# Weights in contiguous slices, prepared in halves, and the rotary product taken from PSUM, in a two-layer attention trunk

## The chip, the core and the metric

The kernel runs on one core of a Trainium2 chip. The metric is the time of one execution in microseconds of device time; the median of three runs is what a change is judged by. The core's engines are PE (matrix multiply), DVE (VectorE), ACT (ScalarE), POOL (GpSimd) and SP (SyncE, which here only issues transfers). Each takes its own instructions strictly in the order in which the program emits them, and waits on semaphores for the others.

## The reference

The input is x, 1024 tokens by 1024 features in float32. Layer A and layer B each add a block to the residual stream, with an RMS norm before and after the block:

```python
# layer A: 16 heads of 64, each query chunk of 64 sees its own and 8 previous chunks
u = rmsnorm(h, a_norm_pre);  q, k, v, g = split(u @ a_w_in, 4)      # 1024 x 4096
o = chunk_band_attention(q, k, v, positions, rel_bias)              # softmax(qk/8 + bias) v
h = h + rmsnorm((o * silu(g)) @ a_w_out, a_norm_post)
# shared keys and values, projected once from the stream
ks, vs = split(rmsnorm(h, kv_norm) @ kv_w, 2);  ks = partial_rope(ks)  # 1024 x 2048
# layer B: 8 heads, two softmax maps each, block-causal
q, g = split(rmsnorm(h, b_norm_pre) @ b_w_in, 2);  q = partial_rope(q)
a = softmax(q0 k0) - lam * softmax(q1 k1)
o = rmsnorm(a @ v, b_subln) * (1 - lam_init)
h = h + rmsnorm((o * silu(g)) @ b_w_out, b_norm_post)
```

partial_rope turns the first 16 of each 64 features: t * cos + swapped(t) * sin.

## The kernel before

**Arithmetic.** Every float32 matrix product is made of three passes over rounded operands: high weights by high data, high weights by low data, low weights by high data. So each operand is cut: a cast gives its high part (`hi_of`, on ACT), a subtraction its low part (`lo_of`, on DVE). A projection group (`mm_group`, L265, L267, L269) is 24 matrix products of 128x128 by 128x512 into one PSUM tile `acc`, of which there are two.

**Order.** Nothing is scheduled by a planner: the class `Ticks` writes the order out by hand. A tick emits first what was put `at` it, then four matrix products of the running stream (`program`), then what was put `after` it or `later`, by rank (0 first) and then by when it was put there. `later(k, f, rank)` means k ticks after the present one, and the rank is 1 where none is given. A projection group takes 6 ticks, and a head pair u takes 8 groups, 48 ticks, in the order `ORDER`: keys and queries of tokens 0 to 511 (K0, Q0), those of tokens 512 to 1023 (K1, Q1), then V0, G0, V1, G1 for values and gates. The attention of pair u begins 24 ticks after the pair's first group and takes 6 ticks for each block of 128 queries in layer B. So blocks 4 to 7 of one pair run beside K0, Q0, K1 and Q1 of the next.

**An attention block in layer B** (`attB_block`): t0 emits the first map's scores (PE L595, one PSUM buffer `sp`), with the mask and the minimum by DVE (`red`, L604, rank 0); t0 + 1 the exponential on ACT (L610); t0 + 3 and t0 + 4 the same for the second map; t0 + 6 the combination of the two maps (`mix`, DVE L936, L937, L939), which stands behind the first `red` of the next block on DVE; t0 + 8 and t0 + 9 transposes on PE (L166, `tp<-ident,s`), each cut by ACT (same tick) and DVE (next tick, rank 0); t0 + 12 and t0 + 13 the product with the values (L970). `close` follows: `c4` (DVE L989) waits for a reciprocal root on POOL.

**The rotary part** (`rope`, L875) is called in the last tick of a K or Q group, which is one tick ahead of the next block's t0. In that tick ACT copies `acc` to `xs` (L883) and SP issues four small transfers from `xs` to `w`, the swapped features. At +2 POOL multiplies `xs` by the cosines in place (L889), at +3 it multiplies `w` by the sines (L890); at +6 DVE adds the two (L891); at +7 ACT makes the high part (L190) and at +8 DVE the low part (L193); for queries SP then sends the parts to the other half of the partitions (L518).

**Weights.** Layer A (`Weights`): ACT issues the load of a 512 KB slice of 128 columns (L216), POOL copies it to its high part (L202), DVE subtracts at the next tick. Layer B's 32 slices are prepared while layer A runs (`Prepared.prepare`, L231): every 10.5 ticks ACT issues a load (L235), at +4 POOL multiplies by the norm's gain (L243), at +6 ACT makes the high part, at +7 DVE the low part, and at +9 SP stores both to DRAM (`wcut`). Loads of weights read 128 columns of a row-major matrix, so each partition's 4 KB come in eight pieces of 512 bytes.

**Output stage of a layer** (`out_stream`): for each of 8 token tiles two groups of 24 products (L780); `finish` computes the norm's factor at its tick, the residual `hres` by DVE at +1 (L813), and in layer A at +2 `next_norm` (`more`): ACT squares and sums `hres` (L186), POOL takes the root, ACT scales (L1026), and PE transposes the tile 8 and 10 ticks later (6 and 7 for the last tile).

Of the kernel before, what the change touches and what calls it, by code (L numbers as in the profile page):

```python
# [11 lines left out]
F32 = mybir.dt.float32  # L12
# [4 lines left out]
ALU = mybir.AluOpType  # L17
# [5 lines left out]
D = 1024  # L23
P = 128
NT = S // P
NC = D // P
# [80 lines left out]
def trunk(ctx, tc, x, positions, a_norm_pre, a_w_in, a_rel_rev, a_w_out, a_norm_post,  # L107
# [5 lines left out]
    adma = nc.scalar.dma_start  # L113
    K = Ticks()
# [4 lines left out]
    o2 = out[0]  # L119
    w_in_a = a_w_in[0].rearrange("(c p) n -> p c n", p=P)  # L120
    w_out_a = a_w_out[0].rearrange("(c p) n -> p c n", p=P)
    w_kv = kv_w.rearrange("(c p) n -> p c n", p=P)
    w_in_b = b_w_in[0].rearrange("(c p) n -> p c n", p=P)
    w_out_b = b_w_out[0].rearrange("(c p) n -> p c n", p=P)
# [64 lines left out]
    def hi_of(src, hi):  # L189
        A.copy(out=hi, in_=src)  # L190
# [9 lines left out]
    def w_split(w):  # L200
        hi, lo = w_tile("whi"), w_tile("wlo")
        G.tensor_scalar(out=hi, in0=w, scalar1=1.0, scalar2=1.0, op0=ALU.mult, op1=ALU.mult)  # L202
        K.later(1, lambda: lo_of(w, hi, lo), 2)
        return hi, lo

    class Weights:
# [5 lines left out]
        def load(self, k, queue=adma):  # L212
            if k < len(self.specs) and k not in self.raw:
                view, cols = self.specs[k]
                self.raw[k] = w_tile("wst").bitcast(F32)
                queue(out=self.raw[k], in_=view[:, :, cols:cols + P])  # L216

# [7 lines left out]
    class Prepared:  # L225
# [5 lines left out]
        def prepare(self, k):  # L231
            view, cols, gain = self.specs[k]
            w = mp.tile([P, D], F32, tag="h", name="w", bufs=4)
            w3 = w.rearrange("p (c n) -> p c n", n=P)
            adma(out=w3, in_=view[:, :, cols:cols + P])  # L235

            def cut():
                hi = mp.tile([P, D], F32, tag="h", name="wh", bufs=4)
                K.later(0, lambda: hi_of(w, hi.bitcast(F32R)))
                K.later(1, lambda: lo_of(w, hi.bitcast(F32R), w.bitcast(F32R)), 2)  # L240
                K.later(3, lambda: [dma(out=wcut[k][:, 0, :], in_=hi), dma(out=wcut[k][:, 1, :], in_=w)])

            K.later(4, lambda: G.tensor_tensor(out=w3, in0=w3, in1=gain.unsqueeze(2).broadcast_to([P, NC, P]),  # L243
                                               op=ALU.mult))
            K.later(6, cut)

# [90 lines left out]
    x_load(1)  # L337
    WA = Weights([(w_in_a, kc * D + u * P) for u in range(8) for kc in (1, 0, 2, 3)])
    WA.load(0, dma)
# [466 lines left out]
    def finish(t, first, second, h, dst, more):  # L806

        def a():
# [9 lines left out]
            if more is not None:  # L818
                K.later(2, lambda: more(t, h))

# [54 lines left out]
    def rope(acc, half, then):  # L875

        cs = slice(half * 512, (half + 1) * 512)
        xs = lp.tile([P, 512], F32, tag="px", name="xs", bufs=3)
        w = rot[swc[0] % 2]
        swc[0] += 1  # L880
# [7 lines left out]
        K.later(0, a)  # L888
        K.later(2, lambda: G.tensor_tensor(out=xs, in0=xs, in1=rot["cos"][:, cs], op=ALU.mult))  # L889
        K.later(3, lambda: G.tensor_tensor(out=w, in0=w, in1=rot["sin"][:, cs], op=ALU.mult))  # L890
        K.later(6, lambda: V.tensor_tensor(out=xs, in0=xs, in1=w, op=ALU.add))  # L891
        then(xs, 6 + 1)

# [12 lines left out]
    def attB(u, base):  # L906
        par = u % 2
        for i in range(NT):
            attB_block(u, par, i, base + 6 * i)

# [112 lines left out]
    def next_norm(t, h):  # L1023
# [3 lines left out]
        for cg in range(2):  # L1027
            K.at(K.pos + (6 + cg if t == NT - 1 else 8 + 2 * cg), lambda cg=cg: transposed(z, cg, uT_dst(R2, t)))

    WB = Prepared([(w, off + u * P, gn) for u in range(8)  # L1030
                   for w, off, gn in ((w_kv, 0, kvg), (w_in_b, 0, bng), (w_kv, D, kvg), (w_in_b, D, bng))])
    OA, OB = OutTiles(otA), OutTiles(otB)
# [147 lines left out]
```

## Time and profile before

| | us |
|---|---|
| median of three runs (1332.06 to 1335.57) | 1332.92 |
| the profiled execution | 1333.15 |
| its span, first to last instruction | 1331.0 |
| PE busy in the span | 1289.9 |
| DVE busy | 834.6 |
| ACT busy | 662.3 |
| POOL busy | 540.2 |

The profiled execution is 2.15 us longer than its span. Engines overlap, so their times do not add up. PE's busy time counts matrix products with modelled ends. Layer A's projections and attention run to about 565 us of the span, its output stage to 689, layer B's projections and attention to about 1200, its output stage to the end.

### The profile page before, as it was taken

The page shows a single profiled execution, that of the slowest core. Times are in us where ns is not written, and L with a number is a line of the kernel's source. Part 1 is how long each engine was busy: PE and PEld are TensorE (multiplying, and loading weights), DVE is VectorE, ACT ScalarE, POOL GpSimd, SP SyncE. Part 2 cuts the span into 40 slices and gives each one's busy share as a digit, 9 for nine tenths or more (in the row PEclk, how much of TensorE's full clock was granted, in tenths as well). Part 3 has the DMA queues.
Part 4 walks back from the last instruction along what each step waited for, and adds up shares of the span by engine and source line. Part 5 has one row for each costly group of instructions (what it writes and reads, how often), then busy time and mean ns, then how long its engine had stood idle before and what let it go on. Part 6 is the DMA issues. An engine that isn't in the chain of part 4 may idle for free.

```text
span 1331.0 us, 20601 instructions
## 1 busy us (share of the span) xinstructions
PE 1289.9 (97%) x6919; PEld 1088.3 (82%) x6919; DVE 834.6 (63%) x1712; ACT 662.3 (50%) x1462; POOL 540.2 (41%) x718
## 2 busy tenths in 40 slices
PE   5999999999999999999998999999999999999998
PEld 5888888888888887887877888888888888888886
DVE  5568866967565655675333575757575757578643
ACT  4355574566454545563343454545454545456311
POOL 2266656656555655542223242424242424242311
PEclk8999999999999999999999999999999999999999
DMA  6588777777877777663464232323232323225353
GB/s 214 137 252 250 243 243 235 228 220 232 250 238 216 241 212 250 194 214 104 142 206 118 71 108 75 109 74 109 74 109 74 104 80 104 79 77 172 98 153 104
DMA packets 160917, 213.46 MB, mean 160 GB/s; under 512 B 13952, under 2 KB 114336, under 8 KB 160800
## 3 DMA queue, kind: packets, MB, share of 16 engines
q1 hardware_dynamic: 83616, 138.08, 33.9%
q10 hardware_dynamic: 77184, 73.95, 18.1%
q8 instruction: 57, 0.93, 0.3%
q14 instruction: 60, 0.49, 0.1%
HBM read 136.47 MB, written 59.79 MB: 147 GB/s over the span
## 4 chain that ended last, share of the span: by engine, by line
PE 52%; DVE 2%; issue 1%; ACT 1%; POOL 1%; DMA 1%; SPq 0%; ACTq 0%; DVEq 0%; POOLq 0%
PE acc L780 12%; PE acc L265 9%; PE acc L267 9%; PE acc L269 9%; PE sp L595 5%; PE av L970 4%; PE tp L166 4%; DVE R L193 1%; DMA sw<-xs 1%; PE av L697 0%; DVE s L604 0%; DVE hres L813 0%; DVE s L939 0%; POOL s L649 0%; ACT R L190 0%
## 5 line engine op out<-in xcount | busy, mean ns | idle before, releaser
L269 PE MATMUL acc<-R,wlo 128*128 128x512 f32 x1008 | 410.7, 407 | 0.0
L267 PE MATMUL acc<-R,whi 128*128 128x512 f32 x1008 | 404.3, 401 | 0.8 <-DVE R L193 0.8
L265 PE MATMUL acc<-R,whi 128*128 128x512 f32 x1008 | 404.4, 401 | 0.2 <-DVE R L193 0.2
L610 ACT ACTIVATE s<-s,st 128x640 f32<-128x640 f32 (+7 forms) x256 | 188.4, 736 | 156.6 <-DVE st L604 155.0
L193 DVE TENSOR_TENSOR R<-tp,R 128x512 fp32r<-128x512 f32 (+3 forms) x304 | 179.5, 603 | 77.9 <-ACT R L190 76.7
L269 PEld LDWEIGHTS acc<-R,wlo 128*128 128x128 f32 x1008 | 190.3, 189 | 33.7
L267 PEld LDWEIGHTS acc<-R,whi 128*128 128x128 f32 x1008 | 190.3, 189 | 33.4 <-DVE R L193 1.1
L265 PEld LDWEIGHTS acc<-R,whi 128*128 128x128 f32 x1008 | 190.5, 189 | 29.3 <-issue 0.4
L190 ACT CAST R<-tp 128x512 fp32r<-128x512 f32 (+3 forms) x304 | 155.6, 515 | 118.1 <-PE tp L166 115.9
L170 POOL TENSOR_TENSOR st<-st,mone 128x1 f32<-128x1 f32 x192 | 121.9, 635 | 200.4 <-ACT s L610 191.7
L595 PE MATMUL sp<-R 128*128 128x256 f32 (+3 forms) x768 | 173.8, 335 | 8.0 <-DVE st L604 6.3
L604 DVE CUSTOM_DVE_ANT_0 s<-sp,mask 128x256 f32<-128x256 f32 (+7 forms) x128 | 96.9, 757 | 132.9 <-PE sp L595 132.7
L780 PE MATMUL acc<-R,ohi 128*128 128x512 f32 x512 | 163.3, 399 | 0.0
L595 PEld LDWEIGHTS sp<-R 128*128 128x128 f32 x768 | 135.8, 189 | 31.4 <-DVE st L604 9.9
L166 PEld LDWEIGHTS tp<-ident,s 128*128 128x128 f32 x768 | 98.1, 141 | 38.7 <-POOL s L649 3.3
L166 PE MATMUL tp<-ident,s 128*128 128x128 f32 x768 | 123.8, 273 | 5.7 <-POOL s L649 3.0
L649 POOL TENSOR_SCALAR s<-s,st 128x640 f32<-128x640 f32 (+4 forms) x128 | 114.8, 897 | 12.6
L179 POOL TENSOR_SCALAR st<-st 128x1 f32<-128x1 f32 x80 | 23.5, 294 | 224.9 <-ACT tt L186 180.6
L889 POOL TENSOR_TENSOR xs<-xs,cos 128x512 f32<-128x512 f32 x32 | 41.3, 1291 | 180.5 <-DMA sw<-xs 136.0
L604 DVE CUSTOM_DVE_ANT_0 s<-sp,bt 128x640 f32<-128x640 f32 (+4 forms) x128 | 83.5, 653 | 47.8 <-PE sp L595 32.4
L780 PEld LDWEIGHTS acc<-R,ohi 128*128 128x128 f32 x512 | 95.0, 189 | 20.1
L780 PE MATMUL acc<-R,olo 128*128 128x512 f32 x256 | 102.8, 402 | 0.0
(125 smaller groups left out, 1692.1 us busy)
## 6 DMA issues: line engine op xcount, KB each, us to landing
bt<-bias_t SPq DMA_DIRECT2D x64, 320.0 KB
R<-R SPq DMA_DIRECT2D x64, 256.0 KB
wcut<-wh SPq DMA_DIRECT2D x32, 512.0 KB
wcut<-w SPq DMA_DIRECT2D x32, 512.0 KB
whi<-wcut ACTq DMA_DIRECT2D x32, 512.0 KB
wlo<-wcut ACTq DMA_DIRECT2D x32, 512.0 KB
wst<-in_a_w_in_dram ACTq DMA_DIRECT2D x29, 512.0 KB
w<-in_kv_w_dram ACTq DMA_DIRECT2D x16, 512.0 KB
```

What stands on the lines that cost most here:

```text
L166: T.transpose(dst, src, ident)
L170: G.tensor_tensor(out=r, in0=a, in1=mone, op=ALU.pow)
L190: A.copy(out=hi, in_=src)
L193: V.tensor_tensor(out=lo, in0=src, in1=hi.bitcast(F32), op=ALU.subtract)
L265: T.matmul(acc, lhsT=hi[:, c, :], rhs=xT(0, c), start=(c == 0), stop=False)
L267: T.matmul(acc, lhsT=hi[:, c, :], rhs=xT(1, c), start=False, stop=False)
L269: T.matmul(acc, lhsT=lo[:, c, :], rhs=xT(0, c), start=False, stop=(c == NC - 1))
L595: T.matmul(sp[:, a:b], lhsT=q[:, l, (i % 4) * P:(i % 4 + 1) * P], rhs=ks[:, head, j0 * P + a - c0:j0 * P + b - c0], start=(l == 0), stop=( ...
L604: V.tensor_tensor_reduce(out=s[:, 0:w], in0=sp, in1=add, op0=ALU.add, op1=ALU.min, scale=-0.125, scalar=BIG, accum_out=mx)
L610: A.activation(s[:, 0:w], s[:, 0:w], AF.Exp, bias=mx, scale=-1.0, accum_out=sums)
L649: G.tensor_scalar(out=s[:, 0:w], in0=s[:, 0:w], scalar1=r, scalar2=0.5, op0=ALU.mult, op1=ALU.mult)
L780: T.matmul(y, lhsT=lhs[:, c, :], rhs=R[:, n * 8 + c, l * 512:(l + 1) * 512], start=(m == 0), stop=(m == 23))
```

## The change

In seven parts: (1) the three input weight matrices are handed to the kernel as slices of 128 columns, laid out so that a partition's 4 KB are one piece; (2) layer A's high weights are made by ACT at the same tick with rank 2, not by POOL; (3) the gain product of the prepared weights is done in two halves at +6 and +7 with rank 2, and the cut follows at +8; (4) `rope` gets a second tile `xc`: DVE multiplies `acc` (PSUM) by the cosines at its first tick with rank 2, POOL multiplies by the sines at +2, DVE adds at +4, and the cut follows at +5 and +6; (5) `xs` and `xc` both come from the ring `px` of three buffers; (6) `next_norm` comes at +5 but for the last tile; (7) block 0 of layer B's first pair starts one tick later.

```diff
-    w_in_a = a_w_in[0].rearrange("(c p) n -> p c n", p=P)
+    w_in_a, w_kv, w_in_b = a_w_in, kv_w, b_w_in
-    w_kv = kv_w.rearrange("(c p) n -> p c n", p=P)
-    w_in_b = b_w_in[0].rearrange("(c p) n -> p c n", p=P)
...
     def w_split(w):
         hi, lo = w_tile("whi"), w_tile("wlo")
-        G.tensor_scalar(out=hi, in0=w, scalar1=1.0, scalar2=1.0, op0=ALU.mult, op1=ALU.mult)
+        K.later(0, lambda: hi_of(w, hi), 2)
         K.later(1, lambda: lo_of(w, hi, lo), 2)
...
-                queue(out=self.raw[k], in_=view[:, :, cols:cols + P])
+                queue(out=self.raw[k], in_=view[n])
...
-            adma(out=w3, in_=view[:, :, cols:cols + P])
+            adma(out=w3, in_=view[n])
...
-            K.later(4, lambda: G.tensor_tensor(out=w3, in0=w3, in1=gain.unsqueeze(2).broadcast_to([P, NC, P]),
-                                               op=ALU.mult))
-            K.later(6, cut)
+            def scaled(half):
+                c = slice(half * 4, half * 4 + 4)
+                G.tensor_tensor(out=w3[:, c, :], in0=w3[:, c, :],
+                                in1=gain[:, c].unsqueeze(2).broadcast_to([P, 4, P]), op=ALU.mult)
+
+            for half in range(2):
+                K.later(6 + half, lambda half=half: scaled(half), 2)
+            K.later(8, cut)
...
             if more is not None:
-                K.later(2, lambda: more(t, h))
+                K.later(2 if t == NT - 1 else 5, lambda: more(t, h))
...
         xs = lp.tile([P, 512], F32, tag="px", name="xs", bufs=3)
+        xc = lp.tile([P, 512], F32, tag="px", name="xc", bufs=3)
...
         K.later(0, a)
-        K.later(2, lambda: G.tensor_tensor(out=xs, in0=xs, in1=rot["cos"][:, cs], op=ALU.mult))
-        K.later(3, lambda: G.tensor_tensor(out=w, in0=w, in1=rot["sin"][:, cs], op=ALU.mult))
-        K.later(6, lambda: V.tensor_tensor(out=xs, in0=xs, in1=w, op=ALU.add))
-        then(xs, 6 + 1)
+        K.later(0, lambda: V.tensor_tensor(out=xc, in0=acc, in1=rot["cos"][:, cs], op=ALU.mult), 2)
+        K.later(2, lambda: G.tensor_tensor(out=w, in0=w, in1=rot["sin"][:, cs], op=ALU.mult))
+        K.later(4, lambda: V.tensor_tensor(out=xc, in0=xc, in1=w, op=ALU.add))
+        then(xc, 4 + 1)
...
-            attB_block(u, par, i, base + 6 * i)
+            attB_block(u, par, i, base + 6 * i + (max(0, 1 - i) if u == 0 else 0))
...
+        if name in ("a_w_in", "kv_w", "b_w_in"):
+            a = a.reshape(NC, P, -1, P).transpose(2, 1, 0, 3)
```

## Rows read from the trace of the kernel before

**Rows 1.** Windows: stretch, us; PE, PEld, DVE, ACT, POOL busy; granted clock; DMA share; GB/s.

```profile
500.00:520.00 20.00, 17.03 (x89) 14.29 (x88) 11.21 (x22) 8.30 (x17) 9.32 (x11) 0.91 0.87 279
600.00:620.00 20.00, 17.69 (x90) 14.57 (x89) 9.93 (x16) 8.00 (x18) 6.56 (x14) 0.91 0.36 112
720.00:740.00 20.00, 18.12 (x85) 14.73 (x83) 9.31 (x29) 8.40 (x23) 5.13 (x7) 0.91 0.25 66
1040.00:1060.00 20.00, 20.00 (x117) 17.22 (x116) 13.70 (x28) 11.32 (x27) 7.86 (x10) 1.00 0.45 146
```

**Rows 2.** ACT's transfer queue, 60:500, then 740:1190: packets, MB, share of 16 engines.

```profile
q10 hardware_dynamic: 56160, 28.32, 23.2%
...
q10 hardware_dynamic: 7715, 28.07, 18.6%
```

**Rows 3.** Timeline, layer A: start, duration, engine; in brackets idle before and releaser.

```profile
378.87 0.87 PE L595 MATMUL sp<-R 128*128 128x384 f32 x4 [1.40 <-DVE st L604]
...
439.27 0.85 PE L595 MATMUL sp<-R 128*128 128x384 f32 x4 [1.26 <-DVE st L604]
...
510.90 1.90 POOL L243 TENSOR_TENSOR w<-w,bng 128x1024 f32<-128x1024 f32 x1 [6.64 <-DMA w<-in_b_w_in_dram]
...
514.26 0.90 PE L166 MATMUL tp<-ident,s 128*128 128x128 f32 x3 [2.97 <-POOL s L649]
```

**Rows 4.** Groups by line: count, then busy us, mean ns; idle before and releasers.

```profile
L202 POOL TENSOR_SCALAR whi<-wst 128x1024 fp32r<-128x1024 f32 x32 | 34.8, 1088 | 22.3 <-PE acc L267 11.4 <-issue 6.0 <-PE acc L269 4.8
L190 ACT CAST wh<-w 128x1024 fp32r<-128x1024 f32 x32 | 33.5, 1048 | 32.4 <-POOL w L243 31.0 <-DMA b<-skew 0.7 <-DMA R<-R 0.6
```

**Rows 5.** Timeline, output stage of layer A.

```profile
607.72 1.06 ACT L186 ACTIVATE z<-hres 128x1024 f32<-128x1024 f32 x1 [3.89 <-DVE hres L813]
...
611.48 0.39 PE L697 MATMUL av<-R 128*128 128x256 f32 x1 [1.97 <-ACT R L190]
```

**Rows 6.** Timeline, layer B's first attention blocks.

```profile
714.61 0.41 PE L595 MATMUL sp<-R 128*128 128x128 f32 x2 [1.56 <-DMA R<-R]
...
720.75 1.29 POOL L889 TENSOR_TENSOR xs<-xs,cos 128x512 f32<-128x512 f32 x1 [4.35 <-DMA sw<-xs]
...
725.27 0.30 PE L166 MATMUL tp<-ident,s 128*128 128x128 f32 x1 [1.88 <-DVE s L939]
```

**Rows 7.** Timeline, layer B, block 6 of pair 4 beside pair 5's Q0 and K1.

```profile
1036.92 1.09 DVE L604 CUSTOM_DVE_ANT_0 s<-sp,mask 128x896 f32<-128x896 f32 x1 [0.76 <-PE sp L595]
...
1038.06 1.04 ACT L610 ACTIVATE s<-s,st 128x896 f32<-128x896 f32 x1 [1.20 <-DVE st L604]
...
1038.88 0.68 DVE L891 TENSOR_TENSOR xs<-xs,sw 128x512 f32<-128x512 f32 x1
...
1040.58 1.26 ACT L190 CAST R<-xs 64x512 fp32r<-64x512 f32 x2 [0.27 <-issue]
...
1040.63 1.23 DVE L604 CUSTOM_DVE_ANT_0 s<-sp,mask 128x1024 f32<-128x1024 f32 x1 [0.87 <-PE sp L595]
...
1042.28 1.15 DVE L939 SCALAR_TENSOR_TENSOR s<-s,st 128x896 f32<-128x896 f32 x1
...
1043.35 1.40 DVE L193 TENSOR_TENSOR R<-xs,R 64x512 fp32r<-64x512 f32 x2
...
1043.66 0.60 PE L166 MATMUL tp<-ident,s 128*128 128x128 f32 x4
```

**Rows 8.** Timeline, the following block 7.

```profile
1046.58 1.23 DVE L604 CUSTOM_DVE_ANT_0 s<-sp,mask 128x1024 f32<-128x1024 f32 x1 [1.45 <-PE sp L595]
...
1049.59 0.28 DVE L604 CUSTOM_DVE_ANT_0 s<-sp,mask 128x128 f32<-128x128 f32 x1
...
1050.31 1.28 DVE L939 SCALAR_TENSOR_TENSOR s<-s,st 128x1024 f32<-128x1024 f32 x1
...
1052.86 0.60 PE L166 MATMUL tp<-ident,s 128*128 128x128 f32 x4
```

**Rows 9.** Waits, whole span: total us, times, longest us.

```profile
DVE yg L803 <- ACT dump L186: 89.8, 32, 4.8
```

More of the change, by code (lines that the diff above doesn't have):

```diff
@@ L213, in load @@
             if k < len(self.specs) and k not in self.raw:
-                view, cols = self.specs[k]
+                view, n = self.specs[k]
                 self.raw[k] = w_tile("wst").bitcast(F32)
-                queue(out=self.raw[k], in_=view[:, :, cols:cols + P])
+                queue(out=self.raw[k], in_=view[n])
         def ready(self, k):
@@ L231, in prepare @@
         def prepare(self, k):
-            view, cols, gain = self.specs[k]
+            view, n, gain = self.specs[k]
             w = mp.tile([P, D], F32, tag="h", name="w", bufs=4)
             w3 = w.rearrange("p (c n) -> p c n", n=P)
-            adma(out=w3, in_=view[:, :, cols:cols + P])
+            adma(out=w3, in_=view[n])
             def cut():
@@ L337, in trunk @@
     x_load(1)
-    WA = Weights([(w_in_a, kc * D + u * P) for u in range(8) for kc in (1, 0, 2, 3)])
+    WA = Weights([(w_in_a, kc * NC + u) for u in range(8) for kc in (1, 0, 2, 3)])
     WA.load(0, dma)
@@ L1028, in next_norm @@
             K.at(K.pos + (6 + cg if t == NT - 1 else 8 + 2 * cg), lambda cg=cg: transposed(z, cg, uT_dst(R2, t)))
-    WB = Prepared([(w, off + u * P, gn) for u in range(8)
-                   for w, off, gn in ((w_kv, 0, kvg), (w_in_b, 0, bng), (w_kv, D, kvg), (w_in_b, D, bng))])
+    WB = Prepared([(w, off + u, gn) for u in range(8)
+                   for w, off, gn in ((w_kv, 0, kvg), (w_in_b, 0, bng), (w_kv, NC, kvg), (w_in_b, NC, bng))])
     OA, OB = OutTiles(otA), OutTiles(otB)
```

## The prediction

> **What bounds the kernel.** I read the windows of 20 us first, then PE's own waits, then the timeline around each of them, and last the timeline of one undisturbed stretch of layer B. In the windows the reader is to see two things. PE is busy through nearly every stretch, in layer B through all 20.00 us while DVE has 13.70, and the granted clock is 1.00, that is 2.4 GHz; so PE's own work sets the time, and a change of the other engines counts only where PE waits for them. And there are three stretches in which PE is not full and the clock reads 0.91 [rows 1]. At 0.91 each loses (1 - 0.91) x 20 = 1.8 us, which I add to the wait that stands ahead of the fall. So the change can win only what PE waits for now, and it loses whatever new wait it makes in front of PE.
>
> **Contiguous slices.** In layer A ACT's queue carries nearly only weights in pieces of 512 bytes: 28.32 MB took 23.2% of all engines' 440 us, 102 us. In layer B the same queue carries pieces of 4 KB: 28.07 MB took 18.6% of 450 us, 84 us [rows 2]. So a slice costs the transfer engines about a fifth less, and there are an eighth as many pieces to be interleaved with SP's. Where a slice is late, POOL stands: 6.64 us at 510.90, and behind it PE waits 2.97 us [rows 3] and the clock falls [rows 1]. Two shorter waits of PE behind a late DVE, 1.40 and 1.26 us [rows 3], I put down to the same chain: ACT's cast waits for POOL's product (31.0 us in all [rows 4]) and DVE waits behind that. Between nothing and all of it I take all, since the landing is what is late: -(2.97 + 1.8 + 1.40 + 1.26) = -7.4.
>
> **High weights on ACT, halves on POOL.** 32 casts of 1.05 us, 33.5 us by the same cast [rows 4], go to ACT, and 34.8 us leave POOL. ACT has 8.3 of 20 us busy in the window that I show of layer A [rows 1], and scores computed at t0 are transposed only eight ticks later; that covers a cast. Bounds are 0 and 33.5; I take 0, and the range carries a tenth, 3.4. The two halves are the same 1.90 us of POOL [rows 3], two ticks later with the cut behind them; the stores on SP move by two ticks too, and nobody reads them before layer B. Without that cover a half could delay POOL's scaling of scores by 0.95; taken as 0.
>
> **Next norm.** ACT's square sum stands 3.89 us in its queue waiting for the residual, the attention's high parts stand behind it, and PE waits 1.97 us for them [rows 5]; then the clock falls [rows 1]. Three ticks later the residual is there before ACT asks for it. Its scale and its eight transposes move along, past no transfer on SP; the last tile, which the next stage needs first, does not move. What is late next is the high part of the last attention batch, behind the 1.06 us sum. Between 0 and -(1.97 + 1.8) I take all: -3.8.
>
> **Rotary part, POOL's side.** 32 products of 1.29 us [rows 6] leave POOL. In layer B POOL waits for the small transfers anyway (4.35 us in that row), so the sine product begins when they land; worth 0 by itself.
>
> **Rotary part, first blocks.** PE waits 1.56 us for the queries' swapped halves and 1.88 us for a combination that stands on DVE behind the addition [rows 6], and the clock falls. An addition two ticks sooner and block 0 one tick later end the first. The second only changes its place: the transfer lands at 720.75, the sine product ends at 722.05, the addition at 722.7, and it now stands ahead of block 0's second `red`. PE needs that single score buffer six ticks after t0, by my count of ticks near 719.8: an estimated wait of 3 us where 3.4 go. I take 0; the ends are -(1.56 + 1.88 + 1.8) = -5.2 and +2.
>
> **Rotary part, steady state.** This is the largest term. DVE gets one product more for each K and Q group, and the low part moves from behind `mix` (+8) to the tick in front of the next block's first `red` (+6), with the new product behind it in that same tick. I work it out for block 6 [rows 7]. DVE's second `red` starts at 1036.92, when PE's scores are there. From there to 1038.88 DVE does it and two low parts of transposes; the addition adds 0.68: 1039.56. ACT ends the exponential at 1039.10; the addition stands ahead of the second low part, so the high parts can begin then, near 1039.2, and the first half of 1.26 is done at 1039.85. Two low parts, 1.40 together: 1041.3. The cosine product costs between 0.62 (`red` from PSUM, 1.09 for 896 columns, scaled to 512) and 0.68 (the addition): 1042.0. So the next `red` starts at 1042.0 and not at 1040.63, 1.4 later, and `mix` behind it too. `mix` ends at 1043.43 now and PE transposes at 1043.66: 0.23 to spare. PE waits 1.2 us. Behind block 7 the same work has 1049.59 - 1046.58 = 3.01 us and not 3.71, so the delay is 2.1; the spare is 1052.86 - 1051.59 = 1.27: 0.8 us [rows 8]. Block 5 (K0's low part, Q0's product) has the same instructions as block 6; I give it 1.2 too. That is 3.2 a pair, and seven pairs have a predecessor whose blocks run beside them: +22.4. Bounds: 0, as DVE has 6.3 of 20 us idle [rows 1], and (1.4 + 1.4 + 2.1) x 7 = 34 without any spare. I take the worked value, because the spare in front of PE is what the rows give.
>
> Can the product run beside ACT's copy of the same PSUM tile? `yg` reads `acc` and the norm's weights and needs nothing of ACT's `dump`, and yet waits for it 32 times, 89.8 us [rows 9]. The Trainium skill, page "PSUM — Partial Sum Buffer", section "PSUM bank collisions raise a hardware error", says that two engines must not read one bank and quadrant at once, so that a kernel has to order them; the trace agrees (89.8 us). It speaks against taking a second reader to PSUM; by it the product begins after ACT's copy, which would follow the high parts and end near 1041.1, before DVE is free, and the sum stays 1344.
>
> **Two buffers of `px`.** A buffer comes back with its low part at +6 or its transfers, and is asked for at +6 at the soonest; 0, or up to a tick if a transfer is late.
>
> **Sum.** 1333.15 for the profiled execution, which is 0.23 above the median: 1333.15 - 7.4 - 3.8 + 0 + 22.4 = 1344.3.
>
> **Rivals.** *Hidden*: DVE absorbs what it gets. For it: PE waits for nothing in that window and DVE is a third idle [rows 1]. Against: that idle time lies in front of `red` (0.87 and 0.76 us [rows 7]), less than the 2.1 us that come in there. It decides if the next `red` still starts with PE's scores. Then 1333.15 - 7.4 - 3.8 = 1322, and 1317 with the first blocks' 5.2. Chance 0.27.
> *Half*: `mix` waits, but by about half, since ACT's high part comes sooner or one block has more spare: 1344 - 11 = 1333. Chance 0.10.
> *Weights no faster*: POOL waits as before, and PE behind it: 1344 + 7.4 = 1352. For it: most slices already land in time. Against: [rows 2]. Chance 0.10. The Trainium skill, page "DMA: Bandwidth & Descriptors", section "Specifications", gives 512 bytes as the size from which transfers go at line rate; by it 4 KB pieces would bring nothing. The trace differs: 102 us against 84 us for the same bytes.
> *Clock*: it fell behind waits of 2.97, 1.97 and 1.88 us, and the window of layer B shows no wait and 1.00 [rows 1, 3, 5, 6]. If one new wait a pair were enough, 7 x 1.8 = 12.6: 1357. Chance 0.05.
>
> **Numbers.** The likeliest case has 0.48 and is 1344, in its own range from 1336 to 1353. Within 0.3% is 4 us, about what a measurement tells from no change. Slower: 0.48 + 0.10 + 0.05, less a little of the first, 0.62; faster 0.27; the same 0.11. The range reaches down to half of the hidden case, 1319, and up to the last, 1357.
>
> **What would show it.** In the changed profile: no DVE `red` of blocks 6, 7 and 0 right after PE's scores, but behind the cosine product; PE waiting about 1 us for `mix` (L939) some 21 times; PE busy below 19 in every second or third window of layer B; no POOL wait of several us for `w`; no ACT wait for `hres` at 607. The prediction is wrong if the windows of layer B still show 20.00, or if layer A keeps its waits.

## The result, and the profile after

The changed kernel takes 1372.03 us, the median of five runs (1370.40 to 1378.16); the kernel before took 1332.98 beside it. The ratio is 1.0293, with an interval of 1.0271 to 1.0315. Slower was forecast, 11 us of it; 39 came.

The windows of the changed kernel (columns as in [rows 1]):

```profile
500.00:520.00 20.00, 20.00 (x112) 17.05 (x111) 12.80 (x26) 11.44 (x22) 11.03 (x14) 1.00 0.72 238
600.00:620.00 20.00, 19.87 (x108) 16.57 (x107) 11.80 (x20) 9.44 (x21) 8.26 (x16) 1.00 0.36 118
720.00:740.00 20.00, 15.49 (x62) 12.27 (x62) 8.56 (x25) 7.46 (x21) 2.31 (x3) 0.83 0.35 107
1000.00:1020.00 20.00, 17.11 (x88) 14.35 (x89) 11.76 (x26) 9.09 (x21) 5.58 (x8) 0.91 0.34 98
```

Against [rows 1], PE is busy through the first two stretches now, but for 0.13 us: the late weights and the late high part of the output stage are gone. The other two are worse: the first blocks of layer B have PE busy for 15.49 us and not 18.12, with a granted clock of 0.83 and not 0.91, and layer B's even stretch, 20.00 before, has windows of 17.11.

Some of the changed kernel's waits (total us, times, longest):

```profile
ACT R L189 <- DVE xc L896: 39.0, 25, 9.4
PE tp L165 <- DVE s L944: 30.5, 23, 2.7
DVE xc L894 <- ACT xs L888: 13.8, 8, 1.8
```

L944 is the last step of `mix` (L939 before); PE now waits for it 23 times, where the kernel before has 3 such waits. ACT stands for 39.0 us with a high part at the head of its queue (L189) that waits for the rotary addition (L896).

The timeline shows how such a wait comes about. This is a block 7 of the changed kernel, the place of [rows 8]:

```profile
1005.42 1.29 POOL L895 TENSOR_TENSOR sw<-sw,sin 128x512 f32<-128x512 f32 x1 [11.91 <-DMA sw<-xs]
1006.75 0.69 DVE L896 TENSOR_TENSOR xc<-xc,sw 128x512 f32<-128x512 f32 x1 [1.70 <-POOL sw L895]
...
1007.47 0.62 ACT L189 CAST R<-xc 64x512 fp32r<-64x512 f32 x1 [1.76 <-DVE xc L896]
...
1008.13 1.41 DVE L192 TENSOR_TENSOR R<-xc,R 64x512 fp32r<-64x512 f32 x2 [0.22 <-ACT R L189]
...
1008.76 0.59 ACT L888 COPY xs<-acc 128x512 f32<-128x512 f32 x1
...
1009.77 0.68 DVE L894 TENSOR_TENSOR xc<-acc,cos 128x512 f32<-128x512 f32 x1
...
1010.37 0.28 DVE L608 CUSTOM_DVE_ANT_0 s<-sp,mask 128x128 f32<-128x128 f32 x1
...
1011.08 1.28 DVE L944 SCALAR_TENSOR_TENSOR s<-s,st 128x1024 f32<-128x1024 f32 x1
...
1012.42 0.79 PE L165 MATMUL tp<-ident,s 128*128 128x128 f32 x4 [2.69 <-DVE s L944]
```

Read it upwards from PE. PE waits 2.69 us for `mix`, `mix` stands behind `red`, `red` behind the cosine product, that behind the low part: this much was forecast. The low part waits for the high part, that for the addition, the addition for the sine product, and POOL starts that only when the small transfers land, at 1005.42. The transfers read what ACT's copy wrote (L888). And the *next* copy, at 1008.76, stands in ACT's queue behind this high part. So each group's copy waits for the transfers of the group before it.

Where the time went, from the starts of landmarks in the timelines: layer A up to the first `yg` (L803 before, L807 after); output stage A from the first to the 16th `yg`; layer B's first blocks from there to the fifth rotary copy (L883 before, L888 after); the rest of layer B to the 17th `yg`. In us, with the experiments below (time: the median, then the ratio to the kernel before beside it, whose median there was 1335.2 to 1336.3, and its interval):

| kernel | time, ratio | layer A | output A | first blocks | rest of B |
|---|---|---|---|---|---|
| before | 1332.98 | 585.1 | 105.0 | 63.7 | 476.8 |
| after | 1372.03, 1.0293 | 586.2 | 100.2 | 72.8 | 516.1 |
| rope_as_before | 1330.09, 0.9950 (0.9931 to 0.9969) | 587.0 | 100.2 | 63.5 | 477.8 |
| cosine_late | 1363.59, 1.0217 (1.0167 to 1.0268) | 585.0 | 100.2 | 72.1 | 501.8 |
| low_behind_mix | 1354.23, 1.0126 (1.0082 to 1.0169) | 587.0 | 100.2 | 69.5 | 497.1 |
| high_and_low_late | 1332.66, 0.9970 (0.9950 to 0.9990) | 585.6 | 100.2 | 63.7 | 481.7 |
| high_ahead_of_copy | 1354.18, 1.0137 (1.0103 to 1.0170) | 585.6 | 100.2 | 68.0 | 497.1 |
| copy_ahead_of_high | 1332.91, 0.9971 (0.9948 to 0.9993) | 586.7 | 100.2 | 62.7 | 481.6 |
| contiguous_only | 1325.31, 0.9928 (0.9912 to 0.9943) | 578.4 | 103.4 | 62.8 | 477.3 |
| contiguous_norm | 1321.71, 0.9894 (0.9875 to 0.9912) | 577.3 | 100.2 | 64.5 | 476.8 |
| contiguous_norm_act | 1325.46, 0.9921 (0.9905 to 0.9937) | 583.0 | 100.2 | 62.2 | 476.8 |
| contiguous_norm_halves | 1327.39, 0.9935 (0.9918 to 0.9951) | 583.0 | 100.2 | 65.1 | 477.2 |
| whole_two_later | 1323.66, 0.9904 (0.9879 to 0.9930) | 582.5 | 100.2 | 65.0 | 476.8 |
| halves_early | 1322.79, 0.9906 (0.9880 to 0.9931) | 577.0 | 100.2 | 64.7 | 477.6 |
| contiguous_norm_2 | 1322.71, 0.9892 (0.9873 to 0.9911) | 579.4 | 100.2 | 65.2 | 476.8 |
| contiguous_norm_halves_2 | 1326.87, 0.9928 (0.9912 to 0.9945) | 583.2 | 100.2 | 64.0 | 477.3 |
| halves_two_sooner | 1317.01, 0.9861 (0.9842 to 0.9881) | 574.1 | 100.2 | 63.5 | 476.9 |
| mended | 1326.41, 0.9938 (0.9921 to 0.9954) | 576.6 | 100.2 | 62.9 | 482.0 |

The change against before, by profile: layer A +1.1, output stage A -4.8, first blocks +9.2, rest of layer B +39.3, output stage B with the end +0.6 (1376.4 - 1275.3 against 1331.0 - 1230.5): +45.4, the difference of the two spans. The changed kernel's profiled run took 1378.16, six above its median.

A stretch is read from one execution: layer A takes 585.0 to 587.0 in the seven kernels that differ in the rotary part alone, and 577.3 and 579.4 in contiguous_norm, run twice, so a difference of some 2 us is no finding. The profile of the kernel before is from the first comparison, where its median was 2 to 3 us lower than beside the experiments; so gains read against that profile are smaller than those by the ratios.

### The profile page after: what moved, and what is told of

The parts are those of the page before. It is cut to its first block, busy times and chain, and to the rows that moved or that the text cites. A ratio compares the mean times of both kernels' runs of the same rounds, so it can differ in the third digit from the quotient of the medians.

```text
span 1376.4 us, 20619 instructions
## 1 busy us (share of the span) xinstructions
PE 1302.9 (95%) x6919; PEld 1091.5 (79%) x6919; DVE 847.6 (62%) x1744; ACT 693.1 (50%) x1494; POOL 456.8 (33%) x686
## 4 chain that ended last, share of the span: by engine, by line
PE 57%; DVE 10%; issue 5%; POOL 4%; DMA 4%; ACT 2%; SPq 2%; ACTq 0%; DVEq 0%; POOLq 0%
PE acc L784 12%; PE acc L273 10%; PE acc L269 9%; PE acc L271 9%; PE tp L165 6%; PE sp L599 6%; DVE R L192 4%; DMA sw<-xs 3%; PE av L701 3%; PE av L975 2%; DVE s L944 1%; DVE s L608 1%; ACT R L189 1%; DVE xc L896 1%; POOL sw L895 1%
## 5 line engine op out<-in xcount | busy, mean ns | idle before, releaser
L189 ACT CAST R<-tp 128x512 fp32r<-128x512 f32 (+3 forms) x304 | 155.0, 515 | 140.2 <-PE tp L165 138.5
L169 POOL TENSOR_TENSOR st<-st,mone 128x1 f32<-128x1 f32 x192 | 132.9, 692 | 277.7 <-ACT s L614 253.8
L895 POOL TENSOR_TENSOR sw<-sw,sin 128x512 f32<-128x512 f32 x32 | 41.2, 1287 | 247.9 <-DMA sw<-xs 208.4
L653 POOL TENSOR_SCALAR s<-s,st 128x640 f32<-128x640 f32 (+4 forms) x128 | 95.4, 745 | 12.6
```

Source lines behind the costliest of these rows:

```text
L169: G.tensor_tensor(out=r, in0=a, in1=mone, op=ALU.pow)
L653: G.tensor_scalar(out=s[:, 0:w], in0=s[:, 0:w], scalar1=r, scalar2=0.5, op0=ALU.mult, op1=ALU.mult)
```

## Experiments: the rotary part

The expectations weigh three theories. The prediction's: the low part and the cosine product stand on DVE in front of `red`, and so delay `mix`. The ring: the high part waits in ACT's queue, the next group's copy stands behind it, and so each group makes the next one late. The third: the cosine product reads the PSUM tile that ACT copies, must wait for the copy, and holds `red` meanwhile.

**rope_as_before.** The whole rotary part put back, the rest as changed.

```diff
-        K.later(0, lambda: V.tensor_tensor(out=xc, in0=acc, in1=rot["cos"][:, cs], op=ALU.mult), 2)
-        K.later(2, lambda: G.tensor_tensor(out=w, in0=w, in1=rot["sin"][:, cs], op=ALU.mult))
-        K.later(4, lambda: V.tensor_tensor(out=xc, in0=xc, in1=w, op=ALU.add))
-        then(xc, 4 + 1)
+        K.later(2, lambda: G.tensor_tensor(out=xs, in0=xs, in1=rot["cos"][:, cs], op=ALU.mult))
+        K.later(3, lambda: G.tensor_tensor(out=w, in0=w, in1=rot["sin"][:, cs], op=ALU.mult))
+        K.later(6, lambda: V.tensor_tensor(out=xs, in0=xs, in1=w, op=ALU.add))
+        then(xs, 6 + 1)
...
-            attB_block(u, par, i, base + 6 * i + (max(0, 1 - i) if u == 0 else 0))
+            attB_block(u, par, i, base + 6 * i)
```

> The changed kernel with the whole rotary part as in the kernel before (cosine product on POOL, addition at +6, high part at +7, low part at +8, block 0 not delayed); weights, halves and next norm as changed. The two traces put the loss into layer B's attention: from the last product of output stage A to the first of output stage B 588.9 us after, 540.4 before, +48.5. Theory (all of that is the rotary part): 1372 - 48.5 = 1323.5, that is 0.993 of before. Rival (the weights' new layout or the casts on ACT also slow layer B): above 1330.

It measured 1330.09, ratio 0.9950. Both stretches of layer B are back at their old lengths (63.5 and 477.8), so all of layer B's loss is the rotary part. The time is above the 1323.5 expected and just past the 1330 of the rival; but the rival was a slower layer B, and that is back. The 48.5 us had been read from the profiled run and taken off the median: 1378.16 - 48.5 = 1329.7. The other parts together are worth only 0.5%, 6.7 us, and by the times the rotary part costs 1.0293 - 0.9950, some 46 us.

**cosine_late.** Only the cosine product one tick later, behind `mix`.

```diff
-        K.later(0, lambda: V.tensor_tensor(out=xc, in0=acc, in1=rot["cos"][:, cs], op=ALU.mult), 2)
+        K.later(1, lambda: V.tensor_tensor(out=xc, in0=acc, in1=rot["cos"][:, cs], op=ALU.mult), 2)
```

> The changed kernel with only the cosine product moved one tick on, behind mix; all else as changed. Theory of the prediction: 0.69 us a block of the delay goes, 2.1 us a pair, 1372 - 15 = 1357. Ring theory: the same or less, since the high part and the copy stay where they are. Third theory (the second reader of the PSUM tile, which must wait for ACT's copy, holds red): most of the 40 us comes back, about 1332.

The rest of layer B gains 14.2 us (516.1 to 501.8), the first blocks almost nothing. By the times the gain is less, 8.4 us by the medians, where the prediction's theory expected 15 and the third 40. So the product's place is not the main cause; the third theory falls.

**low_behind_mix.** Only the low parts back to +8.

```diff
-        K.later(k + 1, lo)
+        K.later(k + gap, lo)
...
-            rope(acc, half, lambda xs, k: split_q(xs, qqB, half, k))
+            rope(acc, half, lambda xs, k: split_q(xs, qqB, half, k, 3))
```

(`split_k` is called likewise.)

> The changed kernel with only the low parts of K and Q put back behind mix (+8 in place of +6); cosine product, addition at +4 and high part at +5 stay. Theory of the prediction (the low part's 1.40 us in front of the next red is the main delay): what is left is the cosine product's 0.69 us against a spare of 0.23, 0.5 us in blocks 5 and 6, so about 1339 and the first blocks' 9 us less or more. Rival (a ring through ACT's queue: the high part waits there for the addition, the next group's copy and its transfers stand behind it, so the next addition comes late again): only blocks 5 and 6 gain, some 2 us a pair, 1372 - 14 = 1358, and block 7 and the first blocks stay as they are.

1354.23: the rest of layer B gains 19.0 and the first blocks 3.3. PE still waits for `mix` in each of blocks 5 to 7, now 0.62, 0.81 and 0.58 us. Of the 19.0, 3.6 are the clock: in the changed kernel's profile two windows of this stretch read 0.91, here none, and (1 - 0.91) x 20 us is 1.8. So the low part is about half of the loss, and the theory of the prediction, 1339, falls as the whole story. The ring theory's 1358 is nearer, but it had expected block 7 and the first blocks to stay. The timeline of a block 7 of this kernel shows what holds it now:

```profile
786.43 0.61 ACT L189 CAST R<-xc 64x512 fp32r<-64x512 f32 x1
...
787.07 0.59 ACT L888 COPY xs<-acc 128x512 f32<-128x512 f32 x1
787.69 0.69 DVE L894 TENSOR_TENSOR xc<-acc,cos 128x512 f32<-128x512 f32 x1 [1.26 <-ACT xs L888]
788.29 0.28 DVE L608 CUSTOM_DVE_ANT_0 s<-sp,mask 128x128 f32<-128x128 f32 x1
...
789.00 1.28 DVE L944 SCALAR_TENSOR_TENSOR s<-s,st 128x1024 f32<-128x1024 f32 x1
...
790.34 0.66 PE L165 MATMUL tp<-ident,s 128*128 128x128 f32 x4 [0.58 <-DVE s L944]
```

DVE is free 1.26 us before it can start the cosine product: the product waits for ACT's copy of the same PSUM tile, and the copy stands behind the high part on ACT. `red` and `mix` follow on DVE.

**high_and_low_late.** High part at +7 and low part at +8, as before; cosine product and addition as changed.

```diff
-        then(xc, 4 + 1)
+        then(xc, 7)
```

> The changed kernel with the high part at +7 and the low part at +8, as before; cosine product on DVE at +0 and addition at +4 stay. Theory of the prediction: the same as with the low part alone, about 1339. Ring theory: the next group's copy no longer stands behind the high part, so block 7 and the first blocks come back too: 1323 to 1333. A third theory (the cosine product from PSUM is itself the delay): at most 15 us better than the changed kernel, about 1357.

1332.66, 21.6 us below the kernel above, with the first blocks at 63.7 and the rest at 481.7. That is inside the ring theory's 1323 to 1333 and below the 1339 of the prediction's. The low part is at the same tick in both kernels, so it is the high part's tick that makes the difference.

**high_ahead_of_copy and copy_ahead_of_high.** The high part at +6, in the tick of the next group's copy, the low part at +7 behind `mix`. The two kernels differ only in the high part's rank in that tick: ahead of what ACT does there, the copies above all, or behind it. In the two traces PE, DVE and POOL run the same instructions in the same order; on ACT the high part changes places with copies of `acc` (L888, L550), and once in the first blocks with an exponential.

```diff
-        then(xc, 4 + 1)
+        then(xc, 6)
...
-        K.later(k, hi)
+        K.later(k, hi, rank)
...
-            rope(acc, half, lambda xs, k: split_q(xs, qqB, half, k))
+            rope(acc, half, lambda xs, k: split_q(xs, qqB, half, k, 0))
```

(rank 2 in place of 0 for the second kernel; `split_k` likewise.)

> The changed kernel with the high part at +6 and the low part at +7 (behind mix), and in that tick the high part queued on ACT ahead of the next group's copy. The order on DVE and PE is that of the next kernel; only two neighbours on ACT change places. Ring theory (copy, four small transfers, sine product, addition, high part, next copy, one after another, 0.6 + 5.3 + 1.3 + 0.7 + 0.6 or more = 8.2 us, where PE needs 5.6 for a group alone): first copies 8.2 us apart, first blocks near 69.5 us, the rest of layer B near 495, that is about 1350. Rival (only DVE's order matters): the same as the next kernel.

> The same with the copy queued ahead of the high part. Ring theory: the ring is open, first copies 5.6 to 6.7 us apart, first blocks near 63.7, the rest of layer B near 482, about 1332. Rival: the same as the kernel above.

1354.18 and 1332.91: 21.3 us for the order of neighbours on ACT. The timelines of layer B's first groups, first with the high part ahead:

```profile
697.90 0.69 DVE L896 TENSOR_TENSOR xc<-xc,sw 128x512 f32<-128x512 f32 x1 [2.36 <-POOL sw L895]
698.62 1.25 ACT L189 CAST R<-xc 64x512 fp32r<-64x512 f32 x2 [3.81 <-DVE xc L896]
699.90 0.59 ACT L888 COPY xs<-acc 128x512 f32<-128x512 f32 x1
...
704.68 1.29 POOL L895 TENSOR_TENSOR sw<-sw,sin 128x512 f32<-128x512 f32 x1 [6.82 <-DMA sw<-xs]
706.01 0.69 DVE L896 TENSOR_TENSOR xc<-xc,sw 128x512 f32<-128x512 f32 x1 [3.38 <-POOL sw L895]
706.73 0.62 ACT L189 CAST R<-xc 64x512 fp32r<-64x512 f32 x1 [6.25 <-DVE xc L896]
...
708.02 0.59 ACT L888 COPY xs<-acc 128x512 f32<-128x512 f32 x1
```

From copy to copy 708.02 - 699.90 = 8.12 us: copy, small transfers until 704.68, sine product 1.29, addition 0.69, the high part's two halves until 708.00, and the next copy. (8.2 was expected, though the terms written there add up to 8.5.) With the copy ahead:

```profile
698.97 0.69 DVE L896 TENSOR_TENSOR xc<-xc,sw 128x512 f32<-128x512 f32 x1 [2.35 <-POOL sw L895]
699.02 0.59 ACT L888 COPY xs<-acc 128x512 f32<-128x512 f32 x1 [3.13 <-PE acc L273]
...
699.69 1.26 ACT L189 CAST R<-xc 64x512 fp32r<-64x512 f32 x2
...
704.62 0.59 ACT L888 COPY xs<-acc 128x512 f32<-128x512 f32 x1 [3.67 <-PE acc L273]
```

The copy waits for PE's projection alone and comes every 5.6 us (704.62 - 699.02). The ring is open, and with it the second cause is shown.

## Experiments: layer A

**contiguous_only.** The kernel before with only the weights' new layout.

```diff
-                queue(out=self.raw[k], in_=view[:, :, cols:cols + P])
+                queue(out=self.raw[k], in_=view[n])
...
-            adma(out=w3, in_=view[:, :, cols:cols + P])
+            adma(out=w3, in_=view[n])
...
+        if name in ("a_w_in", "kv_w", "b_w_in"):
+            a = a.reshape(NC, P, -1, P).transpose(2, 1, 0, 3)
```

> The kernel before with contiguous weight slices alone. Layer A (to the first product of output stage A) took 585.1 us before and 586.2 after, though its late weights no longer show from 345 us on (PE's waits there 6.0 before, 1.6 after), since those from 140 to 345 grew from 4.8 to 11.3. Theory: the slices bring the prediction's 7.4, or less by the clock's share, and the casts on ACT lose 7: this kernel 1326 to 1329, layer A 577 to 580, waits from 140 to 345 about 5. Rival (the slices land sooner but bring nothing, or bring the new waits themselves): 1333, and waits from 140 to 345 of 11.

1325.31, 0.9928, a little under the 1326 to 1329 expected; layer A is 6.7 us shorter by profile, and the ratio makes 9.6 of the whole. ACT's transfer queue in layer A, 60 to 500 us, as in [rows 2]:

```profile
q10 hardware_dynamic: 7794, 28.39, 19.0%
```

7794 packets in place of 56160, the same bytes, 19.0% x 440 = 84 us in place of 102. The waits of [rows 3] shrink: the 2.97 us behind POOL becomes 1.00, the 1.26 is gone, the 1.40 is 1.16. The granted clock reads 1.00 from 500 to 520 us, where it read 0.91.

**contiguous_norm.** The same with the next norm three ticks later.

```diff
-                K.later(2, lambda: more(t, h))
+                K.later(2 if t == NT - 1 else 5, lambda: more(t, h))
```

> The kernel before with contiguous slices and the next norm three ticks later. Output stage A took 104.95 us before and 100.18 after. Theory: 4.8 less than with the slices alone, 1321 to 1324. Rival (the stage's gain came from slices or casts): the same time as with the slices alone.

1321.71, 0.9894, inside the 1321 to 1324 expected; output stage A 100.2 in place of 103.4.

**contiguous_norm_act.** The same with the 32 first-layer casts on ACT.

```diff
-        G.tensor_scalar(out=hi, in0=w, scalar1=1.0, scalar2=1.0, op0=ALU.mult, op1=ALU.mult)
+        K.later(0, lambda: hi_of(w, hi), 2)
```

> The same with the first layer's high weights on ACT. Theory (32 casts of 1.05 us stand in ACT's queue ahead of exponentials and of high parts, DVE's low parts and red wait behind them, and PE for red): layer A 5 to 7 us longer, waits from 140 to 345 about 11, 1327 to 1330. The prediction's value for this part: no difference.

Layer A is 5.7 us longer by profile; by the ratios 0.9921 against 0.9894, 3.6 us, with intervals that overlap a little, and under the 1327 to 1330 expected. PE's waits from 140 to 345 us are 6.0 and not the 11 expected (3.2 without the casts). A place of its timeline, and the same place of contiguous_norm:

```profile
292.61 1.28 ACT L609 ACT_TABLE_LOAD   x1
292.62 1.23 DVE L192 TENSOR_TENSOR wlo<-wst,whi 128x1024 fp32r<-128x1024 f32 x1 [1.64 <-ACT whi L189]
...
295.79 1.62 DVE L192 TENSOR_TENSOR w<-w,wh 128x1024 fp32r<-128x1024 f32 x1 [1.95 <-ACT wh L189]
...
299.70 0.86 PE L594 MATMUL sp<-R 128*128 128x384 f32 x4 [2.33 <-DVE st L603]
```

```profile
290.93 1.23 DVE L192 TENSOR_TENSOR wlo<-wst,whi 128x1024 fp32r<-128x1024 f32 x1 [1.66 <-POOL whi L201]
...
293.15 1.63 DVE L192 TENSOR_TENSOR w<-w,wh 128x1024 fp32r<-128x1024 f32 x1 [1.00 <-ACT wh L189]
...
297.06 0.85 PE L594 MATMUL sp<-R 128*128 128x384 f32 x4 [1.40 <-DVE st L603]
```

While the sine tables are made, ACT loads a function table between a sine and an exponential, 1.28 us each, with the casts or without. For the cast itself DVE stands no longer than it stood for POOL's (1.64 and 1.66 us). But on ACT the cast now comes before a table load, and what follows there is later: DVE waits 1.95 us for the cast of the next layer's weight and not 1.00, and PE 2.33 and not 1.40. These 0.9 us are a third of the 2.8 by which PE's waits grow in this stretch; the rest lies in other places.

**contiguous_norm_halves.** As contiguous_norm, with the second layer's weights scaled in halves and everything behind that two ticks later, as changed.

```diff
-            K.later(4, lambda: G.tensor_tensor(out=w3, in0=w3, in1=gain.unsqueeze(2).broadcast_to([P, NC, P]),
-                                               op=ALU.mult))
-            K.later(6, cut)
+            for half in range(2):
+                K.later(6 + half, lambda half=half: scaled(half), 2)
+            K.later(8, cut)
```

> The same as the second (high weights on POOL) with the second layer's weights scaled in halves. Prediction: no difference, 1321 to 1324. Rival (two ticks later, the halves push the cuts and their stores into other work, or free POOL sooner for the scores): 2 us either way.

Not the prediction's nothing: layer A 5.7 us longer, and 0.9935 against 0.9894. PE's waits from 345 us on fall to 1.5 us, those from 140 to 345 rise from 3.2 to 9.4. One of these:

```profile
222.18 0.36 DVE L450 COPY b<-b 128x384 f32<-128x384 f32 x1 [3.06 <-DMA b<-skew]
...
222.92 1.29 DVE L192 TENSOR_TENSOR R<-tp,R 128x512 fp32r<-128x512 f32 x2
224.12 0.68 DVE L608 CUSTOM_DVE_ANT_0 s<-sp,bt 128x512 f32<-128x512 f32 x1
...
224.87 0.86 PE L599 MATMUL sp<-R 128*128 128x384 f32 x4 [1.38 <-DVE st L608]
```

The bias's transfer on SP is late here: DVE waits for it 3.06 us, where contiguous_norm has 1.57 in this place, and `red` stands behind.

**whole_two_later and halves_early.** The two ticks without the split, and the split without the two ticks.

```diff
-            K.later(4, lambda: G.tensor_tensor(out=w3, in0=w3, in1=gain.unsqueeze(2).broadcast_to([P, NC, P]),
+            K.later(6, lambda: G.tensor_tensor(out=w3, in0=w3, in1=gain.unsqueeze(2).broadcast_to([P, NC, P]),
                                                op=ALU.mult))
-            K.later(6, cut)
+            K.later(8, cut)
```

```diff
+            for half in range(2):
+                K.later(4 + half, lambda half=half: scaled(half), 2)
             K.later(6, cut)
```

> The kernel with contiguous slices and the later next norm, 1321.7, and of the halves part only the two ticks: the whole product at +6 and cast, low part and stores two ticks later. Theory (the ticks cost, since DVE's low part of 1.2 us and SP's stores then meet other work): as slow as with the halves, 1326 to 1328, layer A near 583, PE's waits from 140 to 345 us near 9. Rival (the split into two products costs): 1322.

> The same kernel with the two half products at +4 and +5 and cast, low part and stores where they were. Theory: nothing lost, 1321 to 1323, waits from 140 to 345 near 3 to 4. Rival: 1326 to 1328.

By profile as the theory said: layer A 582.5 with the ticks alone, 577.0 with the split alone, waits from 140 to 345 us 8.3 and 2.7. The times don't tell the two apart: 0.9904 and 0.9906, with intervals of 0.5%. With the split alone the time is as the theory said; with the ticks alone, 1323.66, it misses the 1326 to 1328 forecast, and the profile shows the slowest of its six runs, 1327.63. Inconclusive, so the question was put once more, the other way round.

**halves_two_sooner**, beside contiguous_norm and contiguous_norm_halves run again: the halves as changed, each preparation begun two ticks sooner.

```diff
-        K.after(START + 30 + 21 * k // 2, lambda k=k: WB.prepare(k))
+        K.after(START + 28 + 21 * k // 2, lambda k=k: WB.prepare(k))
```

> The kernel with contiguous slices and the later next norm again, on the chip of the next two, as their measure: 0.9894 of before.

> The same with the halves as changed. If the halves' loss of 5.7 us is real: 4 to 6 us above the kernel before it in this call, layer A near 583 us. If it was the spread of the runs: the same time.

> The halves as changed, but with each preparation begun two ticks sooner, so that cast, low part and stores fall on the ticks of the kernel before, and only the load of the slice and the ring of its buffers move. Theory (the phase of DVE's low part and of what stands beside it costs): as the first kernel, layer A near 577 us. Rival (the split, or the longer life of the buffers): as the second.

0.9892, 0.9928 and 0.9861: the last two intervals don't touch. The windows from 140 to 345 us, first with the halves as changed, then two ticks sooner:

```profile
140.00:345.00 205.00, 195.62 (x1086) 165.29 (x1085) 144.14 (x278) 116.45 (x230) 118.10 (x141) 0.99 0.72 234
```

```profile
140.00:345.00 205.00, 202.47 (x1137) 173.22 (x1136) 150.72 (x290) 122.71 (x242) 123.82 (x146) 1.00 0.74 243
```

PE is busy for 6.9 us more of the stretch; the kernel is the same but for the phase of the preparations. So with the halves the loss is the two ticks; that the ticks cost without the split is shown by profile alone. Which of the moved things carries it, DVE's low part or SP's stores, no run separates, but the traces point at SP's transfers. DVE's waits for the bias's transfer from 140 to 345 us (total, times, longest) are, for contiguous_norm, contiguous_norm_halves and halves_two_sooner:

```profile
DVE b L445 <- DMA b<-skew: 2.9, 2, 1.6
DVE b L450 <- DMA b<-skew: 7.3, 3, 3.3
DVE b L450 <- DMA b<-skew: 1.3, 1, 1.3
```

whole_two_later has 7.2 us of them, halves_early 3.1: they come and go with the two ticks. What holds that transfer longer is not shown.

1317.01 is the best of all kernels here, 1.4% under the kernel before, and better than the theory's "as the first kernel" (layer A 574.1, 577 expected). Whether the split itself gains (0.9861 against 0.9892, intervals that overlap) stays open: the load of each slice also starts two ticks sooner here, and halves_early, which differs from this kernel in that alone, has 0.9906.

**mended.** The changed kernel with both causes undone: copy_ahead_of_high and the preparations two ticks sooner.

> The changed kernel with both found causes undone: the next group's copy ahead of the high part and the low part behind mix (1332.9), and the preparations begun two ticks sooner. Theory: 1332.9 - 4 to 6, 1327 to 1329, 0.994 of before, and still above the first kernel, since the casts on ACT and the cosine product on DVE stay.

1326.41, just under the 1327 to 1329 expected: the edits take about 46 us off the changed kernel. By profile it stands 7 us above halves_two_sooner: the rest of layer B is 482.0 against 476.9, the cosine product, and layer A, with the casts on ACT, 576.6 against 574.1. Those 2.5 us are hardly more than two runs of one kernel differ, so what the casts cost in the old phase stays open.

## Why the prediction was wrong

**Contiguous slices** (-7.4): right, its size in part by luck. Layer A gave 6.7 us alone, and the waits named shrank, but by 3.5 us of 5.6; with the clock's 1.8 that makes 5.3. The rest is not in the term: PE is busy 2.0 us more in the first 140 (125.45 and 123.41). The Trainium skill, page "DMA: Bandwidth & Descriptors", section "Specifications", names 512 bytes as enough for line rate; contiguous_only disagrees as the prediction's estimate did, with 84 us against 102 for the same bytes. *Weights no faster* falls.

**Next norm** (-3.8): right. 3.6 us by the medians behind the slices, 3.2 by profile, and PE is busy for 19.87 us from 600 to 620.

**High weights on ACT, halves on POOL** (0): wrong, though each is a few us. By profile either alone makes layer A 5.7 longer, both together 7.8 (the +1.1 of layer A and the 6.7 that the slices gave); by the ratios 3.6 and 5.5, and both 7.5 (0.9950 against 0.9894). The casts' loss is the less sure, since the intervals overlap. For the casts the step that failed is the cover: it was read in one window, where ACT has 8.3 of 20 us. That is the least of the 25 windows from 60 to 560 us of the same trace, a stretch in which the late slice held everything up; from 280 to 300, where the tables are loaded, ACT has 15.34. For the halves it was that two ticks move nothing that matters: "nobody reads them before layer B" looked at who reads the stores, and not at the rest that moves with them. What is late there is the bias's transfer, for which DVE waits 7.3 us in place of 2.9; through what it is late stays open.

**Rotary, steady state** (+22.4, measured +39.3). The mechanism is right as far as it went: cosine product and low part in front of `red`, then `mix`, then PE, in blocks 5, 6 and 7. Undone step by step, the low part is worth 516.1 - 497.1 = 19.0 us and what is then left, the cosine product with the sooner addition, 481.6 - 476.8 = 4.9, together 23.9 where 22.4 stood, or 20.3 without the 3.6 of the clock. Its division over the blocks was off: PE waits about 0.81, 1.19 and 2.25 (mean of 7, 1.83 to 2.70) and not 1.2, 1.2 and 0.8, 29.7 of the 39.3 in all; that the sum came so near is in part luck. The steps share one spare, so the worth of each depends on the order: the product alone, put behind `mix` first, gave 14.2.

What was missed is 497.1 - 481.6 = 15.5 us: the ring through ACT's queue. The step that failed is the one on POOL's side, with the addition's time behind it: the sine product "begins when they land", with the landing taken from the trace of before. But the high part at +5 waits at the head of ACT's queue for the addition, the next group's copy stands behind it, and so the next landing moves. The prediction looked for what is queued behind the waiting instruction on DVE and not on ACT. Its other sentence on this, that the copy would end before DVE is free, holds with the low part in the way; without it, DVE waits 1.26 us for the copy in low_behind_mix. The Trainium skill, page "PSUM — Partial Sum Buffer", section "PSUM bank collisions raise a hardware error", has two engines' reads of one place put in order by the kernel; the trace agrees (13.8 us in eight waits of L894 for L888), and it matters here, since by that order the late copy reaches DVE as well.

**Rotary, first blocks** (0, upper end +2; measured +9.2). The same ring: no attention runs beside these groups, PE needs 5.6 us for one, the ring 8.1. The timeline of the changed kernel:

```profile
708.67 0.59 ACT L888 COPY xs<-acc 128x512 f32<-128x512 f32 x1
...
715.40 0.41 PE L599 MATMUL sp<-R 128*128 128x128 f32 x2 [3.98 <-DMA R<-R]
...
727.04 0.80 PE L599 MATMUL sp<-R 128*128 128x256 f32 x2 [3.00 <-DVE st L608]
```

The queries' swapped halves were to come sooner; PE waits 3.98 us for them and not 1.56 [rows 6]. Two causes show: 5.2 us between the two kernels that differ in ACT's order (67.96 and 62.72), 3.3 for the low part. Part of both is the clock, which the term held only as a loss to win back: from 700 to 740 us it reads 0.91 and 0.83 here, 1.00 and 0.91 before, 1.00 twice with the copy ahead, so some 3.4 us of the 9.2 (0.17 x 20). The wait for the single score buffer was forecast at 3, and is 3.00; that is luck in its size, since the landing behind it came at 724.79 and not at 720.75, and with the copy ahead there is no such wait. The delay of block 0 by a tick was not tried alone.

**The rivals.** *Hidden* and *Half* fall with the waits for `mix`. *Clock*: it fell in 2 of the 24 windows between 760 and 1240, behind waits of 2.69 and 2.59 us, and not once a pair; one wait of 2.70, at 795.6, left it at 1.00.

**What would show it.** Waits for `mix` came as forecast, three in each of seven pairs; the other two of the 23 (0.22 and 0.56 us, at the end of layer B) the kernel before has too. The waits of [rows 3, 5] went, but layer A did not keep what it gained: PE's waits from 140 to 345 us grew from 4.8 to 11.3.

## What to carry to other kernels

When an instruction is queued sooner and waits, look at what stands behind it on its *own* engine, and whether that starts the next round of the same work: if it does, all latencies of the round add up into a period (8.1 us here, where PE needed 5.6). Then a duration or a landing read in the old trace is no longer a given, and the step must be followed once around.

Where the order on all engines is written by hand in ticks, moving work by two ticks is an edit of its own: it cost as much here as some of the gains, and put back it was worth 0.7%. Each part of a mixed change is worth a run by itself: here two gained 14 us, which the other parts hid.

## What was not expected in the trace

A listed wait understates the delay a little. In copy_ahead_of_high PE's listed waits in the rest of layer B sum to 0.22 us and the clock reads 1.00, yet it takes 4.9 us more than before. The timeline in front of one `mix`, first of contiguous_norm, then of copy_ahead_of_high:

```profile
946.45 0.39 PE L266 MATMUL acc<-R,whi 128*128 128x512 f32 x1
946.68 0.60 PE L165 MATMUL tp<-ident,s 128*128 128x128 f32 x4
```

```profile
956.06 0.39 PE L271 MATMUL acc<-R,whi 128*128 128x512 f32 x1
956.47 0.66 PE L165 MATMUL tp<-ident,s 128*128 128x128 f32 x4
```

A matmul of 512 columns is shown with 0.39 us, but its successor can start 0.23 after it. In the second kernel it starts 0.41 after, 0.18 late, and no wait is listed, since 0.39 are shown as busy. With three blocks a pair and seven pairs there are 21 such steps. In copy_ahead_of_high all 21 transposes start 0.38 to 0.43 us after the matmul before them and 0.06 us after `mix` ends, in contiguous_norm none of them; together they are 3.6 us late, of the 4.9. So in stretches like these the period of a repeated landmark tells more than the sum of the listed waits.
